# A running log-sum-exp over rows: 48 tiles in place of 49, with another order of tile sizes

## The chip, the cores and the metric

The kernel runs on one core of a Trainium2 chip. Times are device microseconds of that core. The time before is the median of three runs, 1260.91 us (1260.88 to 1261.64).

## The reference

The input `x` is 4 x 4096 x 4128 in float32: four batches, 4096 rows, 4128 columns. Each output row is the logarithm of the running sum of exponentials of all rows up to it, column by column:

```python
out[:, 0, :] = x[:, 0, :].copy()
for t in range(1, S):
    mx = np.maximum(out[:, t - 1, :], x[:, t, :])
    out[:, t, :] = mx + np.log(np.exp(out[:, t - 1, :] - mx) + np.exp(x[:, t, :] - mx))
```

The output has the size of the input, so 270.5 MB are read and 270.5 MB are written.

## The kernel before, in words

A tile holds 2 or 3 "blocks" of 128 rows of one batch, all 4128 columns; each of the 128 partitions holds 2 or 3 consecutive rows, so it is contiguous in memory. The list `begin` (lines 149 to 151) gives the sizes for batch 0, `usual` for batches 1 and 2, and `final` for batch 3. A batch has 32 blocks; there are 13 + 12 + 12 + 12 = 49 tiles. Tiles are numbered over all batches, 0 to 48.

Four slots in SBUF hold the tiles in turn: tile t lies in slot t mod 4 (line 158). One slot has room for two blocks only, the other three for three (lines 71 and 72). A tile is loaded into its slot, worked on in place, and stored from it.

The columns of a tile are cut into three chunks of 1376. A `Chunk` has these steps:

- `exp` (line 102): ACT takes the exponential of the chunk's 2 or 3 rows. In the first tile of a batch a small accumulation follows (line 105), which serves a check at the end.
- `sums` (lines 114 and 116): DVE adds up the rows of each partition into the chunk's vector `z`. With three rows it also replaces the second by the sum of the first two (line 114).
- `head` (line 124): PE multiplies `z` with a triangular matrix, so each partition gets the sum of all partitions before it and of the tiles before; the result is in PSUM.
- `add` (lines 133 and 141): DVE adds this to the rows, and leaves the last row's total in `z`, from which the next tile's head takes its carried sum. In the last tile of a batch line 136 takes the place of line 141.
- `log` (lines 146 and 147): ACT takes the logarithm of the rows, first the leading 1 or 2, then the last one from `z`.

Loads (line 88) and stores (line 91) are all issued on SP and go through one queue. Their order is `moves` (lines 166 to 175): four loads, then store 0, and from then on store t followed by load t + 3. Near the end the last two loads follow each other: store n - 5, load n - 2, load n - 1, and then stores n - 4 to n - 1. SP waits for store t until all three logarithms of tile t are done, and for a load until the store that frees its slot has landed.

The order on ACT, DVE and PE is written out by hand. In turn t, ACT has the three logarithms of tile t, and between them the exponentials of tile t + 1, at the places that `usual_turn` (line 179) names; for the turns n - 5 to n - 2 `last_turns` (lines 180 to 185) names others. DVE has `sums` and `add` of tile t, and before the last `add` of a turn the first `sums` of tile t + 1 where the second tuple ends in 1. In the turns n - 5 and n - 4 it does not, and in turn n - 5 no exponential of the next tile is taken ahead. A later instruction on an engine waits for all those before it.

Lists and places are counted from n, the number of tiles, so they move with it:

```python
    last_turns = {
        n - 5: ((0, 0, 0), (0, 0, 0)),
        n - 4: ((0, 2, 3), (0, 0, 0)),
        n - 3: ((2, 3, 3), (0, 0, 1)),
        n - 2: ((2, 3, 3), (0, 0, 1)),
    }
```

Of the kernel before, what the change touches and what calls it, by code (L numbers as in the profile page):

```python
# [7 lines left out]
FP32 = mybir.dt.float32  # L8
# [4 lines left out]
P = 128  # L13
MM = 512
NC = 3
SLOTS = 4
# [5 lines left out]
def kernel(  # L22
# [6 lines left out]
    B, S, D = x.shape  # L29
# [7 lines left out]
    x2 = ctx.enter_context(tc.tile_pool(name="x2", bufs=1))  # L37
    x3 = ctx.enter_context(tc.tile_pool(name="x3", bufs=1))
# [29 lines left out]
    for t in z:  # L68
        nc.gpsimd.memset(t, 0.0)  # L69

    slots = [x2.tile([P, 2, D], FP32, name="x0")]
    slots += [x3.tile([P, 3, D], FP32, name=f"x{k}") for k in range(1, SLOTS)]
    sides = [ppool.tile([P, CH], FP32, name=f"p{k}") for k in range(2)]

    ctx_sched = tc.manual_schedule()
# [70 lines left out]
            nc.scalar.activation(e, e, ACT.Ln)  # L146
            nc.scalar.activation(t.xt[:, r - 1, self.cols], self.z, ACT.Ln)  # L147

    begin = [2, 2, 2, 3, 2, 3, 2, 3, 2, 3, 3, 3, 2]
    usual = [3, 2, 3, 2, 3, 3, 3, 2, 3, 3, 3, 2]  # L150
    final = [3, 3, 3, 2, 3, 3, 3, 2, 3, 3, 2, 2]
    steps = []
    for b in range(B):
        row = 0
# [158 lines left out]
```

## Time and profile before

| | |
|---|---|
| median of three runs | 1260.91 us |
| span of the profiled execution, first to last instruction | 1258.4 us |
| the median above that span | 2.5 us |
| queue of the loads and stores: packets, MB, share | 14112, 541.07, 99.6% |
| mean rate over the span | 430 GB/s |
| DVE busy, ACT busy | 956.2 us, 955.4 us (76% each) |
| PE busy | 602.4 us (48%) |
| load of three blocks, issue to landing (30 of them) | 38.4 us median |
| store of three blocks, issue to landing (30) | 25.0 us median |
| load of two blocks (19), store of two blocks (19) | 33.0 us, 21.6 us median |

The page says of one execution how long each engine was busy, and of the queue how long its packets took. The time of the profiled execution itself is not given apart from its span; the span begins with the first instruction and ends with the last. The time to landing counts the time in the queue behind earlier transfers, which is most of it. In the timeline, a line such as "SPq L91" is an issue on SP, not the transfer; in the chain of waits a "DMA" line runs from issue to landing. In the view by stretches the columns are the stretch, its length, the busy time and count of instructions of each engine, PE's granted clock, the busy share of the DMA engines and GB/s.

### The profile page before, as it was taken

How to read it: one execution, taken by the hardware profiler on the slowest of the kernel's cores; microseconds unless marked ns; L12 is line 12 of the kernel's file. 1: busy time of each engine (PE TensorE's matmuls, PEld its weight loads, DVE VectorE, ACT ScalarE, POOL GpSimd, SP SyncE). 2: the span in 40 equal slices, each digit the busy share in tenths (PEclk: the TensorE clock that was granted, in tenths of full speed). 3: DMA queues.
4: the chain of work that ended last, by engine and by line, in shares of the span. 5: the costliest groups of instructions: out<-in, count | busy, mean ns of one | idle time of the engine just before them, and what ended most of it. 6: DMA issues, size and time to landing. Idle time of an engine off the chain costs nothing.

```text
span 1258.4 us, 3228 instructions
## 1 busy us (share of the span) xinstructions
PE 602.4 (48%) x884; PEld 233.1 (19%) x884; DVE 956.2 (76%) x548; ACT 955.4 (76%) x466; POOL 4.6 (0%) x14
## 2 busy tenths in 40 slices
PE   3654454453535455345364535634535553463361
PEld 1221121121212122112121212211211211121120
DVE  3997696795967699579596679957957976795792
ACT  6987687786976699578697668866968966896792
POOL 1000000000000000000000000000000000000000
PEclk9877776676677667666676666766766776676676
DMA  9999999999999999999999999999999999999998
GB/s 403 420 439 426 432 436 428 432 437 429 439 425 438 430 437 433 436 435 427 440 422 436 436 432 434 434 430 435 437 428 437 431 435 431 434 437 433 432 435 354
DMA packets 14131, 541.28 MB, mean 430 GB/s; under 512 B 1568, under 2 KB 1568, under 8 KB 1568
## 3 DMA queue, kind: packets, MB, share of 16 engines
q1 hardware_dynamic: 14112, 541.07, 99.6%
q8 instruction: 7, 0.11, 0.0%
q14 instruction: 12, 0.10, 0.0%
HBM read 270.53 MB, written 270.53 MB: 430 GB/s over the span
## 4 chain that ended last, share of the span: by engine, by line
DMA 69%; ACT 14%; DVE 13%; PE 1%; issue 1%; SPq 0%; ACTq 0%; DVEq 0%
DMA x<-in_x_dram 52%; DMA out_dram<-x 17%; ACT x L102 6%; DVE x L133 5%; ACT x L146 5%; DVE z L116 3%; ACT x L147 3%; DVE z L141 3%; DVE x L114 2%; PE p L124 1%; SPq L91 0%; DVE z L136 0%; ACTq L146 0%; ACTq L254 0%; SPq L88 0%
## 5 line engine op out<-in xcount | busy, mean ns | idle before, releaser
L124 PE MATMUL p<-z,carried 128*128 128x512 f32 (+1 forms) x810 | 551.8, 842 | 544.3 <-DVE z L116 544.3
L102 ACT ACTIVATE x<-x 128x4128 f32<-128x4128 f32 (+1 forms) x147 | 468.0, 3187 | 219.7 <-DMA x<-in_x_dram 219.7
L124 PEld LDWEIGHTS p<-z,carried 128*128 128x128 f32 x810 | 213.4, 280 | 882.2 <-DVE z L116 648.3
L133 DVE TENSOR_TENSOR x<-p,x 128x2752 f32<-128x2752 f32 (+1 forms) x147 | 361.9, 2462 | 6.2 <-PE p L124 6.2
L146 ACT ACTIVATE x<-x 128x2752 f32<-128x2752 f32 (+1 forms) x147 | 300.6, 2045 | 63.5 <-DVE z L141 58.5
L114 DVE TENSOR_TENSOR x<-x 128x1376 f32<-128x1376 f32 x90 | 142.9, 1588 | 216.5 <-ACT x L102 216.5
L116 DVE TENSOR_TENSOR z<-x 127x1376 f32<-127x1376 f32 x147 | 233.9, 1591 | 53.8 <-ACT x L102 49.4
L141 DVE TENSOR_TENSOR z<-x 128x1376 f32<-128x1376 f32 x135 | 215.0, 1592 | 4.6
L147 ACT ACTIVATE x<-z 128x1376 f32<-128x1376 f32 x147 | 196.0, 1334 | 0.0
L124 PE MATMUL p<-z,below 128*128 128x512 f32 (+1 forms) x72 | 50.4, 864 | 87.4 <-DVE z L116 87.4
L124 PEld LDWEIGHTS p<-z,below 128*128 128x128 f32 x72 | 19.6, 289 | 117.7 <-DVE z L116 78.8
L136 DVE CUSTOM_DVE_ANT_0 z<-x 128x1376 f32<-128x1376 f32 x12 | 19.1, 1592 | 0.4
L105 ACT ACTIVATE spare<-x,tiny 1x1376 f32<-1x1376 f32 x12 | 17.3, 1442 | 0.5
L69 POOL MEMSET z<- 128x1376 f32 x3 | 3.7, 1241 | 0.0
L105 ACT ACTIVATION_READ_ACCUMULATOR spare<-x,tiny 1x1 f32 x12 | 2.2, 186 | 0.0
L247 PE MATMUL good<-ones,low 128*1 128x1 f32 x2 | 0.2, 164 | 3.8 <-DVE low L245 3.8
L34 ACT ACT_TABLE_LOAD x1 | 1.3, 1283 | 0.8 <-PEq L297 0.8
L136 DVE DVE_READ_ACCUMULATOR2_ANT probe<- 128x1 f32 x12 | 1.0, 83 | 0.0
L247 PEld LDWEIGHTS good<-ones,low 128*1 128x1 f32 x2 | 0.1, 80 | 4.8 <-DVE low L245 4.8
L249 DVE TENSOR_SCALAR flag<-good 1x1 int32<-1x1 f32 x1 | 0.1, 148 | 0.3 <-PE good L247 0.3
L51 POOL TENSOR_SCALAR_AFFINE_SELECT carried<-below 128x128 f32<-128x128 f32 x1 | 0.3, 290 | 0.0
L45 POOL TENSOR_SCALAR_AFFINE_SELECT below<-below 128x128 f32<-128x128 f32 x1 | 0.3, 285 | 0.0
(13 smaller groups left out, 1.6 us busy)
## 6 DMA issues: line engine op xcount, KB each, us to landing
x<-in_x_dram SPq DMA_DIRECT2D x30, 6192.0 KB, 38.4
out_dram<-x SPq DMA_DIRECT2D x30, 6192.0 KB, 25.0
x<-in_x_dram SPq DMA_DIRECT2D x19, 4128.0 KB, 33.0
out_dram<-x SPq DMA_DIRECT2D x19, 4128.0 KB, 21.6
```

The lines of the kernel that those rows point to most:

```text
L34: nc.scalar.preload_act_table_set("natural_log_exp_and_others")
L69: nc.gpsimd.memset(t, 0.0)
L102: nc.scalar.activation(e, e, ACT.Exp)
L105: nc.scalar.activation(spare, t.xt[0:1, 0, self.cols], ACT.Relu, bias=tiny, scale=-1.0, accum_out=short[:, k:k + 1],)
L114: nc.vector.tensor_tensor(out=e[1], in0=e[0], in1=e[1], op=ALU.add)
L116: nc.vector.tensor_tensor(out=self.z[0:n], in0=e[r - 2][0:n], in1=e[r - 1][0:n], op=ALU.add,)
L124: nc.tensor.matmul(pt[:, a:b], lhsT=w, rhs=self.z[:, a:b], start=True, stop=True,)
L133: nc.vector.tensor_tensor(out=e, in0=base, in1=e, op=ALU.add)
L136: nc.vector.tensor_tensor_reduce(out=self.z, in0=ends[0], in1=ends[1], scale=1.0, scalar=0.0, op0=ALU.add, op1=ALU.add, accum_out=probe[:, ...
L141: nc.vector.tensor_tensor(out=self.z, in0=ends[0], in1=ends[1], op=ALU.add)
L146: nc.scalar.activation(e, e, ACT.Ln)
L147: nc.scalar.activation(t.xt[:, r - 1, self.cols], self.z, ACT.Ln)
```

## The change

The slot for two blocks is now the second of the four, where it was the first. The lists of sizes are new; batch 0 has 12 tiles in place of 13, so there are 48 tiles, 32 of three blocks and 16 of two, where there were 30 and 19. Batch 3 has the same list as batches 1 and 2. The run begins with tiles of 2, 2, 3, 3 blocks (before: 2, 2, 2, 3) and ends with 3, 2, 3, 2 (before: 3, 3, 2, 2). Nothing else is changed; n is 48, so the special turns at the end are those of tiles 43 to 46, where they were those of tiles 44 to 47.

```diff
-    slots = [x2.tile([P, 2, D], FP32, name="x0")]
-    slots += [x3.tile([P, 3, D], FP32, name=f"x{k}") for k in range(1, SLOTS)]
+    slots = [x3.tile([P, 3, D], FP32, name="x0"), x2.tile([P, 2, D], FP32, name="x1")]
+    slots += [x3.tile([P, 3, D], FP32, name=f"x{k}") for k in range(2, SLOTS)]
...
-    begin = [2, 2, 2, 3, 2, 3, 2, 3, 2, 3, 3, 3, 2]
-    usual = [3, 2, 3, 2, 3, 3, 3, 2, 3, 3, 3, 2]
-    final = [3, 3, 3, 2, 3, 3, 3, 2, 3, 3, 2, 2]
+    begin = [2, 2, 3, 3, 3, 2, 3, 3, 3, 2, 3, 3]
+    usual = [3, 2, 3, 3, 3, 2, 3, 3, 3, 2, 3, 2]
+    final = usual
```

## The prediction

> **What bounds the kernel now.** I read the page from its third part upward: first which queue is busy, then whether anything else ever ends a wait, then the issues on the queue near both ends.
>
> ```profile
> PE 602.4 (48%) x884; PEld 233.1 (19%) x884; DVE 956.2 (76%) x548; ACT 955.4 (76%) x466; POOL 4.6 (0%) x14
> q1 hardware_dynamic: 14112, 541.07, 99.6%
> ```
>
> The one queue that carries all loads and stores has packets in work for 99.6% of the span. No compute engine is over 76%. So the bytes set the time, and the other engines matter only where they leave the queue without a transfer. The view by stretches says where that is (the last columns are the share of the DMA engines and GB/s):
>
> ```profile
> 0.00:10.00 10.00, 0.00 (x0) 0.00 (x0) 0.00 (x0) 1.28 (x1) 4.64 (x14) 1.00 0.84 337
> 600.00:610.00 10.00, 6.16 (x9) 2.02 (x7) 8.40 (x8) 9.86 (x6) 0.00 (x0) 0.54 0.96 416
> 1230.00:1240.00 10.00, 4.11 (x8) 1.29 (x6) 6.52 (x11) 5.77 (x5) 0.00 (x0) 0.69 0.96 416
> 1240.00:1250.00 10.00, 0.00 (x0) 0.00 (x0) 0.00 (x0) 0.00 (x0) 0.00 (x0) 0.50 1.00 433
> ```
>
> Only the first microseconds are below the usual rate; up to 1250 us the queue is full, with all compute over by 1240. The issues on SP at the end (start, length, count), and the chain of waits there:
>
> ```profile
> 1147.18 0.33 SPq L91 DMA_DIRECT2D out_dram<-x  x1
> 1163.66 24.92 SPq L88 DMA_DIRECT2D x<-in_x_dram  x2
> 1189.55 50.68 SPq L91 DMA_DIRECT2D out_dram<-x  x4
> ...
> 1134.38 44.32 DMA x<-in_x_dram
> 1178.72 3.65 ACT x L102
> 1182.40 1.60 DVE x L114
> 1184.02 1.60 DVE z L116
> 1185.67 4.48 PE p L124 x6
> 1190.17 3.04 DVE x L133
> ```
>
> The reader is to see that the last four stores, tiles 45 to 48, leave one by one as tiles get ready (1189.55, 1213.10, 1228.04, 1239.89 in the timeline of SP). Their completions in the trace, issue plus time to landing, are 1222.74, 1237.38, 1247.12 and 1257.13; before them load 46 landed at 1178.70, store 44 at 1188.18, load 47 at 1197.88, load 48 at 1208.09. In the queue a store of three blocks therefore takes 14.65 and one of two 9.75. When store 48 was issued, store 47 had 7.2 us to go; stores 46 and 47 had 9.6 and 9.3 in front of them. Those are the margins that the change spends.
>
> **The change part by part.** Transfers: 30 three-block and 19 two-block tiles become 32 and 16. The blocks are 128 both times, so the queue's work is the same: 3 x 9.75 - 2 x 14.65 = -0.05 us for each direction. I take 0.
>
> Here a rule speaks for a gain. The Trainium skill, page "DMA: Bandwidth & Descriptors", section "Anatomy of one DMA — SWDGE (gpsimd) path", gives a fixed cost of about 2.0 us for each transfer besides its bytes; two tiles' worth of transfers fewer (98 to 96) would then save about 2 x 2.0 = 4.0 us, estimated from that page. The steps of 14.65 and 9.75 disagree for a queue that is never empty, since their ratio is that of the bytes.
>
> Compute: three two-block chunks become two three-block ones. On DVE a two-block chunk takes 1.51 (L116) + 3.13 (L133, L141) = 4.64 from start to start, a three-block one 3.13 + 4.59 = 7.72; 2 x 7.72 - 3 x 4.64 = 1.5, for three chunks 4.6 us more. ACT: two blocks 2.39 + 2.49, three 3.54 + 3.64; 0.3 less per chunk, 0.8 in all. Both lie under the queue's 99.6%, except in the tail.
>
> Start: tile 2 grows by a block. Store 0 waits for nothing of tile 2 and stays at 38.04. Store 1 has two exponentials of tile 2 ahead of it on ACT, 2 x 1.15 longer: 52.73 + 2.3 = 55.0. Load 3 lands 4.9 later, near 53.1, and store 0 near 62.9, so store 1 has 7.9 in front of it, load 4 (slot 0 is free at 62.9) 9.8. Store 2, three blocks, comes some 23 to 25 us after store 1, as store 3 did after store 2 before (92.87 - 70.28 = 22.6): near 79, while load 4 ends near 87.5. Nothing runs dry: 0 us. The first load is two blocks as before, so nothing starts sooner.
>
> Middle: a store leaves a fixed stretch after the next tile's load has landed (load 43 at 1095.30, chain to 1110.64: 15.3) and then 9.0 us of the queue are left. The tightest new place is store 11, three blocks before the first tile of batch 1, whose accumulations on ACT (1.44 + 0.19 each, two of them ahead of the last logarithm) take 3.2 off: 5.8 left. 0 us.
>
> End: this is where I put the cost. The order of work in the last turns counts from the end, so the sizes that meet it change from 2, 3, 3, 2, 2 to 3, 3, 2, 3, 2. Take load 46, now three blocks and the last but one. Behind it in the queue stand load 47 (2), stores 44 to 47 (3, 2, 3, 2), twelve blocks; behind load 47 before stood load 48 and stores 45 to 48, also twelve. So load 46 lands when that one did, 1197.88. Store 46 must be on the queue when store 45 is done: 1197.88 + 10.21 (as load 48) + 14.65 + 9.75 = 1232.5.
>
> When is store 46 issued? Distances from start to start, from rows of this tail. Exponential of tile 46, chunk 0, at 1197.90; its L114 3.68 later, 1201.58; L116 +1.62, 1203.20. Next on DVE stands the last addition of tile 45, because that turn takes one sum of the next tile first: L133 1204.71, L141 1206.33, free at 1207.84. Chunk 1: L114 1207.84, L116 1209.46. Addition of chunk 0: L133 1210.97, L141 +3.05, 1214.02, free 1215.53. Sum of chunk 2: 3.13, 1218.66. Addition of chunk 1: 4.55, 1223.21. Sum of tile 47, chunk 0 (one L116): 1224.72. Addition of chunk 2 ends at 1224.72 + 3.05 + 1.59 = 1229.36. ACT meanwhile: logarithm of chunk 0 1215.65 (3.64), two exponentials of tile 47 (4.78) to 1224.07, logarithm of chunk 1 to 1227.71, third exponential to 1230.10. The last logarithm, 2.38 + 1.34, is done at 1233.82 and store 46 is issued at 1233.86. PE's heads take up to 4.96 and start at 1204.95, 1211.2 and 1218.9, each 0.8 us or more before they are needed. One condition: ACT must have finished the logarithm of tile 45's chunk 0 by 1197.88; counted forward from load 43, with an idle PE's 4.1 to 5.0 in two heads, it ends near 1196.5.
>
> So the queue is empty when store 46 arrives. The price of a start on an empty queue is seen once, bounded both sides: load 0 landed 12.25 us after its issue, two blocks, 2.5 above the 9.75 in the queue; the least is what no start can avoid, 1.0 from issue to the first packet (0.80 to 1.81 in the trace) and 0.45 from last packet to completion (1256.67 to 1257.13). That first load was the run's first transfer of any kind and went the other way, so neither row is near a store in mid-run, and I take the middle, 2.0. Store 46 lands at 1233.86 + 14.65 + 2.0 = 1250.5, against 1247.1 on a full queue: 3.4 us late (2.8 to 3.9 at the ends). Store 47: tile 47 has 12.7 us of DVE work left after 1229.4 (two L116, three additions); with a PE head in between and the last logarithm, 2.6, it is issued near 1246.5, four before 1250.5. It lands 10.0 later at 1260.5; behind that the span has 1.3 (1257.13 to 1258.42). Span 1261.8 against 1258.42: +3.4. The median 1260.91 stands 2.5 above the profiled span; that part is unchanged, so 1264.3.
>
> **The rivals.** First, the tail is in time: not slower. It decides at 33 us from load 46's landing to store 46's issue, where I count 36.0. For it: tile 46 before, of the same size in the same kind of turn, took 34.4 (1178.70 to 1213.10), with 1.0 of that waiting for PE. Against: the addition of tile 45, 3.1 us, did not stand in it then. Time: 1260.9.
>
> Second, the chain is longer: the two conditions at 1196.5 and 1197.88 change places because heads on an idle PE take 4.96 instead of 4.1, or heads are late by as much in the tail. One to two us more: 1266.
>
> Third, every transfer pays for itself and two tiles fewer gain. Load 0's 2.5 us is the only such row; 2 x 2.5 off gives 1255.9. The full queue's steps speak against it. The rule cited above would be this case and make it 1256.9.
>
> **How the numbers follow.** Store 46 late: 70%, between 1262.4 and 1265.9. Longer chain: 14%. In time: 13%. Gain: 3%. A measurement here tells about 0.2%, 2.5 us, so slower means above 1263.43; the forecast's own lower end is under it in about a sixth of its cases, 12 points. Slower 58 + 14 = 72; same 12 + 13 = 25; faster 3. For 8 in 10 the range reaches up into the longer chain, 1266.3, and down to 1261.5, where part of the "in time" case lies; drift of the slowest of the sixteen engines, whose last completion came 5.6 us after the first's (1251.55 to 1257.13), is in it with half a microsecond.
>
> **What would show it.** Right: in the tail SP issues store 46 some 36 us after load 46 landed; the DMA share dips for about 2 to 4 us near 1233 to 1236, and nowhere else after the start; the completions of the sixteen engines lie closer together in the last store than 5.6 us, as they start together. Load 46 landing at 1197 to 1198.5 shows start and middle as free. Wrong: no dip, or a dip at the border of batch 0, or an issue of store 46 before 1232.

## The result and the profile after

The changed kernel takes 1264.97 us (median of six runs, 1264.30 to 1266.35) against 1260.89 (six runs, 1260.32 to 1261.64). The ratio is 1.0034, 95% interval 1.0023 to 1.0044: slower by 0.34%, 4.1 us. The profiled execution is the slowest of the six; its span is 1264.5 us, those of the others 1262.6 to 1264.3. What it has over the median is told apart below.

The page of the changed kernel, engines and queue:

```profile
PE 601.4 (48%) x866; PEld 232.1 (18%) x866; DVE 959.8 (76%) x545; ACT 954.4 (75%) x457; POOL 4.6 (0%) x14
q1 hardware_dynamic: 13824, 541.07, 99.2%
```

The same bytes, 288 packets fewer (one load and one store, with their completions), DVE 3.6 us more and ACT 1.0 less, where 4.6 more and 0.8 less were forecast. The share of the queue falls from 99.6% to 99.2%, which is 5 us of the longer span. The view by stretches has them in one place (the last two columns are the DMA share and GB/s):

```profile
0.00:10.00 10.00, 0.00 (x0) 0.00 (x0) 0.00 (x0) 1.28 (x1) 4.64 (x14) 1.00 0.87 343
600.00:610.00 10.00, 4.75 (x8) 1.98 (x8) 8.44 (x6) 9.73 (x5) 0.00 (x0) 0.82 1.00 433
1220.00:1230.00 10.00, 7.10 (x10) 2.96 (x11) 9.93 (x6) 10.00 (x7) 0.00 (x0) 0.71 0.84 363
1230.00:1240.00 10.00, 6.15 (x12) 2.48 (x11) 9.93 (x8) 8.58 (x5) 0.00 (x0) 0.84 0.42 182
1240.00:1250.00 10.00, 2.22 (x6) 0.64 (x4) 4.62 (x10) 5.18 (x4) 0.00 (x0) 0.67 1.10 476
```

Between 1230 and 1240 the DMA engines are busy for 0.42 of the time, where it was 0.96, while DVE is busy for 9.93 of the 10 us. The queue waits for store 46, and that store for the work on tile 46, most of it on DVE. The dip begins in the ten microseconds before: a transfer has sixteen completions, one for each DMA engine, and "landed" means the last of them; the first engine was through with store 45 at 1227.52. The issues on SP, and the chain of waits in the tail:

```profile
1160.09 24.76 SPq L88 DMA_DIRECT2D x<-in_x_dram  x2
1193.30 55.04 SPq L91 DMA_DIRECT2D out_dram<-x  x4
...
1197.12 1.35 ACT x L146
1198.47 1.24 ACT x L147
1199.71 3.54 ACT x L102
1203.27 1.60 DVE x L114
1204.90 1.59 DVE z L116
1206.49 1.51 DVE x L133
1208.03 1.59 DVE z L141
1209.62 1.51 DVE x L114
1211.18 0.41 issue
1211.59 1.59 DVE z L116
```

Store 45 landed at 1233.93; store 46 was issued at 1236.02, 2.1 us after the queue had become empty, and landed at 1252.72. Behind a full queue a store of three blocks lands 14.65 after its predecessor, which would be 1248.58: 4.1 us are lost here. This is the size of the difference of the medians. The chain shows why it was late: from the load of tile 46 on, DVE works with hardly a gap, and the chain begins with a logarithm of tile 45 (L146, L147) that ends at 1199.7, after load 46 had landed (1199.03).

The spans differ by 6.1, which is more. In completions, against the place before with as many blocks behind it: load 46 landed 1.15 later than load 47 did (1199.03, 1197.88), the three transfers up to store 45 took 0.3 more, store 46 lost 4.14, store 47 took 10.91 in place of 10.01, and the span's end came 0.4 sooner after it. Without the logarithm of one chunk (a run below) load 46 landed at 1197.83, which speaks for scatter of that execution.

### The profile page after: what moved, and what is told of

It reads as the page before. It is cut to its first block, busy times and chain, and to the rows that moved or that the text cites. A ratio compares the mean times of both kernels' runs of the same rounds, so it can differ in the third digit from the quotient of the medians.

```text
span 1264.5 us, 3172 instructions
## 1 busy us (share of the span) xinstructions
PE 601.4 (48%) x866; PEld 232.1 (18%) x866; DVE 959.8 (76%) x545; ACT 954.4 (75%) x457; POOL 4.6 (0%) x14
## 3 DMA queue, kind: packets, MB, share of 16 engines
q1 hardware_dynamic: 13824, 541.07, 99.2%
## 4 chain that ended last, share of the span: by engine, by line
DMA 66%; DVE 16%; ACT 13%; PE 2%; issue 1%; SPq 0%; ACTq 0%; DVEq 0%
DMA x<-in_x_dram 43%; DMA out_dram<-x 24%; DVE x L133 6%; ACT x L102 6%; ACT x L146 4%; DVE z L116 4%; DVE z L141 3%; DVE x L114 2%; ACT x L147 2%; PE p L124 2%; DVE z L136 0%; ACT spare L105 0%; SPq L91 0%; ACTq L254 0%; ACTq L146 0%
## 5 line engine op out<-in xcount | busy, mean ns | idle before, releaser
L133 DVE TENSOR_TENSOR x<-p,x 128x2752 f32<-128x2752 f32 (+1 forms) x144 | 365.8, 2540 | 6.8 <-PE p L124 6.8
L146 ACT ACTIVATE x<-x 128x2752 f32<-128x2752 f32 (+1 forms) x144 | 303.5, 2108 | 67.6 <-DVE z L141 62.2
L114 DVE TENSOR_TENSOR x<-x 128x1376 f32<-128x1376 f32 x96 | 152.4, 1588 | 225.1 <-ACT x L102 225.1
L116 DVE TENSOR_TENSOR z<-x 127x1376 f32<-127x1376 f32 x144 | 229.2, 1591 | 49.2 <-ACT x L102 44.5
L141 DVE TENSOR_TENSOR z<-x 128x1376 f32<-128x1376 f32 x132 | 210.2, 1593 | 4.5
L147 ACT ACTIVATE x<-z 128x1376 f32<-128x1376 f32 x144 | 192.0, 1334 | 0.0
```

Of the source, the lines that this page charges most:

```text
L114: nc.vector.tensor_tensor(out=e[1], in0=e[0], in1=e[1], op=ALU.add)
L116: nc.vector.tensor_tensor(out=self.z[0:n], in0=e[r - 2][0:n], in1=e[r - 1][0:n], op=ALU.add,)
L133: nc.vector.tensor_tensor(out=e, in0=base, in1=e, op=ALU.add)
L141: nc.vector.tensor_tensor(out=self.z, in0=ends[0], in1=ends[1], op=ALU.add)
```

## The experiments

Theory: all of the loss is the late store 46. Rivals: the loss comes with the new start, the middle or the place of the slot; with 48 tiles or more of three blocks as such; or a late last store costs its whole lateness.

**The end alone.** The kernel before, with the sizes at the end as in the change:

```diff
-    final = [3, 3, 3, 2, 3, 3, 3, 2, 3, 3, 2, 2]
+    final = [3, 3, 3, 2, 3, 3, 3, 2, 3, 2, 3, 2]
```

> The kernel before in all but the list of batch 3, which now ends with 3, 2, 3, 2 (its last five sizes were 2, 3, 3, 2, 2 and become 2, 3, 2, 3, 2). 49 tiles, the start and the place of the two-block slot as before. Theory (the last-but-one store comes after the queue has run empty): store 47 is issued some 36 to 37 us after load 47 has landed, while the queue has 34.5 us behind that load, and the time rises by 3 to 4.5 us, to 1264 to 1265.4. Rival (the time is lost in the start, the middle or by the place of the slot): 1260.9, no change.

Measured: 1264.13 us, ratio 1.0025 (1.0016 to 1.0034). Load 47 landed at 1198.02, store 47 was issued 36.1 later at 1234.09, 1.6 after store 46 had landed. The stretch with the empty queue, of this kernel:

```profile
1230.00:1240.00 10.00, 6.66 (x12) 2.76 (x12) 9.93 (x9) 7.64 (x6) 0.00 (x0) 0.83 0.57 244
```

The order 3, 2, 3, 2 makes the loss by itself, with 49 tiles and the old start; it loses 3.15 us where the changed kernel loses 4.1, and the intervals overlap, so whether something else adds the rest is not told by this run. The chain of waits of this kernel begins with the load, not with ACT, and here the 36 us are met:

```profile
1163.90 34.11 DMA x<-in_x_dram
1198.04 3.65 ACT x L102
1201.72 1.60 DVE x L114
1203.34 1.59 DVE z L116
```

**Start and middle, first try.** The changed kernel with another batch 3:

```diff
-    final = usual
+    final = [3, 2, 2, 3, 2, 2, 3, 3, 3, 2, 3, 2, 2]
```

> The changed kernel in all but the list of batch 3, which has 13 tiles and ends with 3, 2, 3, 2, 2; 49 tiles again, first batch in 12, two-block slot second. The last-but-one load has two blocks again. Theory (tail alone): no empty queue, 1260.9 within 0.7. Rival (start, middle or slot): 1264 to 1265.

Measured: 1263.01 us, ratio 1.0019 (1.0009 to 1.0028). Neither theory nor rival. The last four stores were in time (4.0 us or more of the queue in front of each), but in the middle of batch 3 the rate dips:

```profile
1040.00:1050.00 10.00, 6.40 (x10) 2.57 (x11) 8.44 (x6) 10.00 (x7) 0.00 (x0) 0.66 0.92 396
1050.00:1060.00 10.00, 5.33 (x12) 2.22 (x11) 9.52 (x8) 10.00 (x7) 0.00 (x0) 0.92 0.98 401
```

Store 39 was issued at 1044.52, 3.6 us before load 41 had landed on the last of the sixteen DMA engines and 1.0 after it had on the first. So this list had made a weak place of its own: a large tile behind two small ones. It did not answer the question, and raised another: the slowest engine never ran dry there, so why did the time rise? The next run is about the first question, the last of this section about the second.

**Start and middle, second try.**

```diff
-    final = usual
+    final = [3, 2, 2, 2, 3, 2, 3, 3, 3, 2, 3, 2, 2]
```

> Start and middle of the changed kernel once more (first batch in 12, two-block slot second), with another batch 3 of 13 tiles: 3, 2, 2, 2, 3, 2, 3, 3, 3, 2, 3, 2, 2. The run with 3, 2, 2, 3, 2, 2 in its place had store 39 with only 3.6 us of the queue left, so its fast engines waited there. Here no store should have less than 8.5 us left before the tail. Theory (start and middle cost nothing): 1260.9 within 0.7. Rival (first batch, slot or a longer list cost 2 us): 1263.

Measured: 1261.43 us, ratio 1.0003 (0.9994 to 1.0012). The median hides two groups: five of the eleven executions took 1260.1 to 1260.6 us, five 1262.3 to 1262.7, and one the 1261.43. The traced one is the longest, and what it loses is not lost in the start or the middle: load 36, the first of batch 3, landed at 934.90, and in the kernel before the load with as many blocks up to it (load 37) at 934.47. It is lost in the new batch 3, where loads 39 and 42 took 10.74 and 15.40 us from the landing in front of them, against 9.7 and 14.6 on a full queue. Each stands behind a store (36, 39) that had 2.1 and 1.7 us in front of it on the first engine. So the first batch in 12 tiles, the moved slot and the two batches that follow cost nothing that can be told from no change, but this run shows it by its trace and its shorter group, not by its median alone.

The margins, that is what the queue still has in front of a store when it is issued, were smaller than expected: the least ahead of the tail was 6.8 us (store 39), and in the tail stores 46 to 48 had 4.1 to 4.9. At stores 46 and 48 the first engines had run dry there: the sixteen completions, 5.5 us apart before, came within 3.6 and 2.8. With only stores behind them that cost nothing to be seen.

**Less work in the tail.** The changed kernel, two instructions left out:

```diff
         def log(self):
             t, r = self.t, self.t.r
+            if t.n == n - 2 and self.c == NC - 1:
+                return
```

> The changed kernel without the logarithm of the last chunk of tile 46 (both instructions, 3.7 us of ACT); that chunk of the output is left unfinished. Theory: store 46 is issued when DVE is done with the tile, some 32.5 us after load 46 has landed, before the queue is empty at 34.4; nothing runs dry and the time goes back to 1261 within 0.8, though only 3.7 us of one engine's work are gone. Rival (start, middle or slot): stays at 1264.5 to 1265. Rival (the last tile's own work sets the end): 3.7 us less at most by way of ACT, with the queue still empty for 1 to 4 us around 1235.

Measured: 1260.66 us, ratio to the kernel before 1.0000 (0.9991 to 1.0009). Store 46 was issued at 1228.26, 30.4 after load 46, with 4.5 us of the queue left. That is 2.1 sooner than expected: without the logarithm the store waits only for the last addition to the rows (L133, over at 1228.2), not for L141 after it. The rate in the stretch is back:

```profile
1230.00:1240.00 10.00, 6.85 (x12) 2.70 (x12) 9.93 (x9) 4.01 (x4) 0.00 (x0) 0.83 0.97 418
```

Start, middle, tiles and their order are those of the changed kernel. With store 46 in time, nothing of the 4.1 us is left in the median. Two of the eleven executions took 1262.6 and 1262.7, like the longer group above; the trace is of the shortest, so what these two lost is not known. Load 36 landed at 934.07 here, 0.4 before its counterpart in the kernel before; the four traces with these first 36 tiles have it at 934.07 to 935.46, the changed kernel's last. This kernel also has 48 tiles, 32 of three blocks, so their number as such is not slower.

**A late store, on the kernel before.** Idle instructions on ACT ahead of the last logarithm, seven and then three:

```diff
         def log(self):
             t, r = self.t, self.t.r
+            if t.n == n - 1 and self.c == NC - 1:
+                for _ in range(7):
+                    nc.scalar.activation(spare, self.z[0:1, :], ACT.Relu)
```

> The kernel before with seven idle instructions on ACT (one partition, 1376 elements, about 1.25 us from start to start, 8.7 us in all) ahead of the last chunk's logarithm of tile 48, so that only the last store is later. Before, it had 5.9 us to spare on the slowest of the sixteen engines: 7.2 less 0.45 of completion less 0.84 from issue to first packet. Theory (a late store costs only what is over the margin): 8.7 - 5.9 = 2.8, time 1263.4 to 1264.6. Rival (any microsecond late in the tail counts): +8.7, 1269.6. Rival (the end does not hang on the issue of the last stores): 1260.9.

Measured: 1264.07 us, ratio 1.0023 (1.0014 to 1.0032). The seven took 9.63 us; store 48 was issued at 1250.46, 1.4 after store 47 had landed. The stretch from 1240 to 1250 of this kernel:

```profile
1240.00:1250.00 10.00, 0.00 (x0) 0.00 (x0) 0.00 (x0) 9.84 (x8) 0.00 (x0) 0.50 0.35 152
```

> As the run with seven idle instructions ahead of tile 48's last logarithm, with three (4.1 us). That is under the margin of 5.9 us. Theory (a late store costs what is over the margin): 1260.9 within 0.5. Rival (the last stores set the end at any lateness): +4.1, 1265.

Measured: 1260.87 us, ratio 1.0000 (0.9991 to 1.0009). Store 48 was issued at 1244.13, 4.1 us before store 47 had landed. Some 4 us of lateness cost nothing, 9.6 cost 3.1 (the sum by the margin would be 9.6 - 5.9 = 3.7). So lateness counts only from some point on, and that point lies between an issue 4.1 us before the queue is empty and one 1.4 us after.

**48 tiles with another order.**

```diff
-    slots = [x3.tile([P, 3, D], FP32, name="x0"), x2.tile([P, 2, D], FP32, name="x1")]
-    slots += [x3.tile([P, 3, D], FP32, name=f"x{k}") for k in range(2, SLOTS)]
+    slots = [x3.tile([P, 3, D], FP32, name=f"x{k}") for k in range(SLOTS - 1)]
+    slots.insert(2, x2.tile([P, 2, D], FP32, name="x3"))
...
-    begin = [2, 2, 3, 3, 3, 2, 3, 3, 3, 2, 3, 3]
-    usual = [3, 2, 3, 3, 3, 2, 3, 3, 3, 2, 3, 2]
-    final = usual
+    begin = [3, 2, 2, 3, 3, 3, 2, 3, 3, 3, 2, 3]
+    usual = [2, 3, 2, 3, 3, 3, 2, 3, 3, 3, 2, 3]
+    final = [3, 3, 2, 3, 3, 3, 2, 3, 3, 3, 2, 2]
```

> 48 tiles in another order: the two-block slot is the third, batch 0 is 3, 2, 2, 3, 3, 3, 2, 3, 3, 3, 2, 3, batches 1 and 2 are 2, 3, 2, 3, 3, 3, 2, 3, 3, 3, 2, 3, batch 3 is 3, 3, 2, 3, 3, 3, 2, 3, 3, 3, 2, 2, so the run ends with 3, 3, 2, 2 as before. Theory (the order at the end, not the number of tiles): the slowest engine never waits, 1260.9 within 0.9. Rival (48 tiles or 32 of three blocks are slower as such): 1264 to 1265.

Measured: 1263.89 us, ratio 1.0025 (1.0016 to 1.0035). The expectation missed, and not for the rival's reason. The issues on SP at the start of this kernel, and its stretches there and in the tail:

```profile
0.80 2.12 SPq L88 DMA_DIRECT2D x<-in_x_dram  x4
52.86 15.30 SPq L91 DMA_DIRECT2D out_dram<-x  x2
...
50.00:60.00 10.00, 5.67 (x10) 2.58 (x11) 8.50 (x6) 10.00 (x6) 0.00 (x0) 0.79 0.76 327
1230.00:1240.00 10.00, 7.11 (x14) 2.55 (x13) 8.90 (x8) 7.72 (x6) 0.00 (x0) 0.84 0.95 411
```

The four loads had landed by 52.61, and store 0 was issued at 52.86: with three blocks in the first tile, its work ends too late, and the queue is empty at the start; the DMA share is 0.76 in that stretch. Store 1 too had only 1.1 us in front of it. In the tail, which ends with 3, 3, 2, 2, all stores were in time with 4.6 us or more. So 48 tiles are not slow at the end as such, as the run without one logarithm says too; but a kernel of 48 tiles that does all of its work and loses nothing was not found.

**Engines that run dry while the slowest does not.** The kernel before, with a delay far from both ends:

```diff
         def log(self):
             t, r = self.t, self.t.r
+            if t.n == 41 and self.c == NC - 1:
+                for _ in range(5):
+                    nc.scalar.activation(spare, self.z[0:1, :], ACT.Relu)
```

> The kernel before with five idle instructions on ACT (1.36 us each, 6.8 in all) ahead of the last logarithm of tile 41, far from both ends. Store 41 had 9.0 us of the queue in front of it on the slowest of the sixteen engines and 4.4 on the first; now 2.2 and none. Theory A (only the slowest engine counts, it never runs dry): 1260.9. Theory B (engines that run dry are thrown into step with the others, and all of them then lose about 1 us at the next changes between loads and stores, as at the end of load 3 and after store 39 of the last study): 1 to 3 us more, 1262 to 1264, with a smaller spread of the sixteen completions afterwards.

Measured: 1263.15 us, ratio 1.0017 (1.0008 to 1.0026); in the range of theory B. Issue of store 41, and the stretches behind it, of this kernel; the last three lines are the same stretches of the kernel before:

```profile
1093.13 0.33 SPq L91 DMA_DIRECT2D out_dram<-x  x1
...
1090.00:1100.00 10.00, 0.08 (x2) 0.07 (x1) 3.56 (x4) 10.00 (x5) 0.00 (x0) 0.66 0.89 381
1100.00:1110.00 10.00, 6.56 (x9) 2.82 (x10) 9.93 (x5) 9.31 (x5) 0.00 (x0) 0.67 0.94 380
1110.00:1120.00 10.00, 7.27 (x10) 2.52 (x8) 9.90 (x7) 9.11 (x5) 0.00 (x0) 0.50 0.97 375
...
1090.00:1100.00 10.00, 4.83 (x7) 1.52 (x6) 8.72 (x6) 8.41 (x4) 0.00 (x0) 0.80 1.04 451
1100.00:1110.00 10.00, 4.99 (x7) 1.88 (x7) 9.90 (x7) 9.26 (x5) 0.00 (x0) 0.66 0.95 410
1110.00:1120.00 10.00, 6.27 (x9) 2.41 (x10) 9.93 (x5) 8.20 (x5) 0.00 (x0) 0.72 1.00 434
```

Load 43 landed between 1090.51 and 1095.45 on the sixteen engines, so only the early ones waited. On the last engine store 41 landed at 1110.12, where it was 1109.99 before: the slowest had lost nothing yet. But the sixteen now ended within 0.6 us of each other (4.7 before), the rate stayed at 375 to 381 GB/s over 30 us (part of it is the wait of the early engines itself; the ten microseconds after had 471), load 44 took 10.90 on the last engine in place of 9.67, and store 48 landed at 1259.01 in place of 1257.13. That the engines' being in step is what makes them lose time is argued from this, not shown by itself.

## Why the prediction was right

**Queue work, start, middle.** Right, each near its number. Store 1 was issued at 55.59 (55.0), load 3 landed at 53.26 (53.1), store 0 at 63.02 (62.9), store 2 was issued at 79.81 (79) with 8.6 us to spare. Store 11, the tightest in the middle, had 6.7 (5.8). The run with start and middle alone has a ratio of 1.0003, and its trace is 0.4 us behind the kernel before at the first load of batch 3.

**Load 46 at 1197.88.** 1199.03 in the profiled execution, 1197.83 in the run without one logarithm.

**36.0 us to the issue of store 46.** It took 37.0, and the condition named beside it failed: the logarithm of tile 45's chunk 0 ended at 1199.70, not near 1196.5, so ACT came to tile 46 0.6 us after its load. The other 0.4 is the pause ahead of L116 at 1211.59 in the chain above, "issue" there: the profile shows nothing that it waited for, and its cause stays open. The late logarithm is the second rival, in small. All other distances held to a tenth; in the run with the end alone, where ACT was ready for the load, it took 36.1.

**2.0 us for a start on an empty queue.** The sum came out, the term only on the last engine of this execution, which is partly luck. Store 46 landed 16.70 after its issue on the last engine, 2.05 over the 14.65 of a full queue, but 15.84 on the first, 1.2 over. In the run with the end alone both are 15.9 and 16.0, so the start costs 1.2 to 1.4, just under the lower of my two bounds (1.45), in which 1.0 stood for the time from issue to first packet where 0.84 was measured; the rest of the 2.05 fell on some engines only, later in that transfer. A packet of store 46 that took 0.6 us longer than the others is in the trace. The Trainium skill, page "DMA: Bandwidth & Descriptors", section "Anatomy of one DMA — SWDGE (gpsimd) path", has about 2.0 us fixed for a transfer on the path that GpSimd issues; here SP issues all of them. The traces have 1.2 to 2.05 on an empty queue and none on a full one: the run without one logarithm, with 96 transfers and no late store, takes 1260.66 us, ratio 1.0000 to the kernel with 98.

**Store 46 late by 3.4.** 4.1: the issue came 1.0 later against the load and the queue ran empty 0.3 later, so the gap between them is 0.7 longer, and the start cost 2.05 where 2.0 was put in. The median of 1264.97 is 0.7 over the 1264.3 of the forecast.

**Store 47 near 1246.5, in time.** 1248.00, with 4.7 us of the queue in front of it. In time.

**What would show it.** The dip is at 1227 to 1236 alone; it begins at 1227.5 and not near 1233, because the first engine runs dry before the last, by which the forecast went. The sixteen completions of store 46 lie within 0.9 us, as they start together (those of store 45: 6.4), those of the last store within 2.0.

**The rivals.** "In time" fell with the 37 us. The gain from fewer transfers did not appear; the prediction speaks there of two tiles fewer, but it is one tile, a load and a store. The point from which lateness counts, which the first rival put at 33 us from the load, was not measured as such: an issue 30.4 us after the load was free, one after 36.1 was not.

## What to carry to other kernels

Where one queue bounds the kernel, list for each store how much of the queue is in front of it when it is issued; a change of sizes or order is worth what it does to the smallest of these margins. In the tail, with only stores behind, a margin of 4 us on the last engine cost nothing. Ahead of the tail count it on the first engine too: there stores with 2.3 and 3.6 us in front of them on the last engine and none on the first went with 2.4 and 2.0 us more. The weakest places here were the first store, which must come before the first loads are through, and the last two, where the load just before the last has little behind it and its whole tile has still to be computed: keep that tile small. A large tile behind two small ones was a third. Changing the sizes also moves every special order that is counted from the end, so the tail has to be worked out anew even if "only" the start was meant.

## What the runs showed of the hardware that was not expected

The sixteen DMA engines drift apart: their completions of one transfer lie 0.5 us apart at the start and 5 to 7 at the end of a run with a full queue. The last one sets the end.

A queue that runs dry on the early engines alone costs time too, here 2.4 us for a delay that left the slowest engine busy; the run with a weak place in the middle shows the same, 2.0 us. Afterwards the completions lie within 0.6 us and 2.4 us. The store behind the late one in the tail does not show this loss (9.75 us from first completion to first completion in the changed kernel, 9.73 in the run with the end alone, as on a full queue), so it may belong to changes between loads and stores; that was not tried apart.

A store that starts on an empty queue has its first packets 0.84 us after its issue (1236.02 to 1236.86).
